# Two transformer blocks on 256 tokens: the residual and its products turned to tokens on partitions

## The chip, the cores and the metric

One core of one Trainium2 chip runs the whole program in one launch. The metric is device microseconds (us) from the first to the last instruction of an execution, the median of several executions. Inputs and outputs are float32 in HBM.

## The reference, cut to what matters

256 tokens of width 2048 (`D`) pass through two blocks. The first has two layers, the second one layer with adaptive modulation.

```
# block 1, layer i = 0, 1
h = rms_norm(x, norm_mix[i])
mix = attention(h)  (i == 0)  or  recurrent(h)  (i == 1)     # both end in a product with a 2048 x 2048 weight
x = x + mix
h = rms_norm(x, norm_ffn[i])
x = x + (silu(h @ w_gate) * (h @ w_up)) @ w_down             # 2048 -> 5632 -> 2048

# attention: qkv = h @ w_qkv (16 query heads, 4 key heads, 4 value heads of 128),
#   q, k = rope(rms_norm(head) * gain), softmax over all 256 tokens, o @ w_o

# block 2 (sh, sc, gt from c @ w_ada)
h = rmsnorm(x, g_pre_mix) * (1 + sc_m) + sh_m
proj = h @ w_in                                              # window attention and a state space model
merged = [rmsnorm(attn, g_attn_out), rmsnorm(ssm, g_ssm_out)]
x = x + (1 + gt_m) * rmsnorm(merged @ w_out, g_post_mix)
h = rmsnorm(x, g_pre_ffn) * (1 + sc_f) + sh_f
up = causal_conv(h @ w_up)                                   # 2048 -> 2 x 5632
x = x + (1 + gt_f) * rmsnorm((gelu(gate) * val) @ w_down, g_post_ffn)
```

## The kernel before

All weights, some 666 MB, are read once, in tiles of 512 KB, and every product is exact to about float32: a weight tile `wr` is split into a rounded half `wh` (a cast on ScalarE) and a rest `wl` (a subtraction on VectorE), the input into `hi` and `lo` the same way, and TensorE adds up wh·hi + wh·lo + wl·hi in PSUM. A queue on SP loads tiles up to four ahead, and the split runs up to two tiles ahead of TensorE. TensorE works through the tiles in the order of a plan (`plan_weights`). The order on each engine is that of the program text, moved by a scheduler with priorities, and an engine carries out its own list strictly in order.

There are two ways to run a tile. In `gemm` the **weight is stationary**: a tile holds four blocks of 128 input features by 256 output features; each 128 x 128 weight is loaded into the array and the tokens stream past, 512 columns for `wh` (256 tokens, `hi` and `lo` side by side) and 256 columns for `wl`. That is 8 instructions of 512 columns and 8 of 256, and the result has features on partitions. In `gemm_t` the **input is stationary**: 128 tokens by 128 features are loaded, and 512 columns of the weight stream past; a tile is 12 instructions of 512 columns, and the result has tokens on partitions. Both stream 6144 columns for each tile. Before the change only gate and up of the first two feed-forward networks (FFN) use `gemm_t`; their result is turned by transposes on TensorE (`psh`) to become the input `hc` of the down product.

The residual is kept as eight tiles `x[0..7]` of 128 features x 2 x 256 tokens. Products into the residual (`proj_x`: `wo`, `wd`, `wrout`) run in eight blocks of 256 output features. Blocks 0 and 1 run as a pair, tile by tile in turn, into both of the two PSUM buffers `pg`; the last block, 7, is `narrow`: it runs in 256-column instructions, three for each weight block, so that the result needs one addition per half. The other blocks leave two halves of 256 columns to be added to `x` by VectorE.

A norm over features is a sum over partitions here: ScalarE squares (`stat_add`), GpSimd adds up the squares, TensorE multiplies by a matrix of ones into `psn`, and the reciprocal root is taken on 128 x 256 elements by ScalarE (Ln, Exp) and VectorE. In the attention every head block needs the same (`pss`). At the two norms inside block 2, `post` and `modulate` work over the eight tiles `x[j]`; `mix`, `ff` are the products' outputs, `gg_m`, `gg_f`, `gp_m`, `gp_f` the gains, and `hh` is the split input of the next product.

Of the kernel before, what the change touches and what calls it, by code (L numbers as in the profile page):

```python
# [8 lines left out]
F32 = mybir.dt.float32  # L9
F32R = mybir.dt.float32r  # L10
AF = mybir.ActivationFunctionType
# [5 lines left out]
T = 256  # L17
# [9 lines left out]
    ("q_gain", 1), ("k_gain", 1),  # L27
# [28 lines left out]
class Build:  # L56
    def __init__(self, ctx, tc, A, stop=None):
        self.tc, self.nc, self.A, self.stop = tc, tc.nc, A, stop
# [8 lines left out]
        self.mods = {}  # L67
# [12 lines left out]
    def const(self, name, shape, dtype=F32):  # L80
        return self.cp.tile(list(shape), dtype, tag=name, name=name, bufs=1)

# [91 lines left out]
    def plan_weights(self):  # L174
# [24 lines left out]
        for b in range(12):  # L199
            add(("qkv", b), [A["wqkv"][b]], 0, 16)  # L200
# [70 lines left out]
    def gemm(self, key, xs, kbase=0, narrow=False):  # L271
# [5 lines left out]
        for bi, a, b in seq:  # L277
            wh, wl = self.next_w()
            steps = [(m, kc, xs[kc - kbase], slice(m * 128, (m + 1) * 128)) for m in range(2) for kc in range(a, b)]
            for m, kc, x, c in steps:  # L280
                if narrow:
                    self.mm3(ps[bi][:, m, 0:256], wh[:, kc - a, c], wl[:, kc - a, c], x,
                             kc == lo, kc == hi - 1)
                else:
                    self.mm(ps[bi][:, m, :], wh[:, kc - a, c], x.rearrange("p a t -> p (a t)"),
                            start=(kc == lo), stop=False)
            for m, kc, x, c in steps if not narrow else ():
                self.mm(ps[bi][:, m, 0:256], wl[:, kc - a, c], x[:, 0, :],
                        start=False, stop=(kc == hi - 1))
            self.tick()  # L290
        return ps

    def gemm_t(self, key, xs):
# [6 lines left out]
        for _, a, b in seq:  # L300
            wh, wl = self.next_w()
            for kc in range(a, b):
                for t in range(2):
                    c = slice(t * 128, (t + 1) * 128)
                    self.mm(ps[:, t, :], xs[kc][:, 0, c], wh[:, kc - a, :], start=(kc == lo), stop=False)
                    self.mm(ps[:, t, :], xs[kc][:, 1, c], wh[:, kc - a, :], start=False, stop=False)
            for kc in range(a, b):
                for t in range(2):
                    c = slice(t * 128, (t + 1) * 128)
                    self.mm(ps[:, t, :], xs[kc][:, 0, c], wl[:, kc - a, :], start=False, stop=(kc == hi - 1))  # L310
            self.tick()
# [21 lines left out]
    def stat(self, n, pairs=8):  # L333
        return {"acc": None, "n": n, "left": pairs, "sq": [], "one": False}

    def stat_add(self, s, x, direct=False):

        sq = self.slot("sq")
        if s["left"] == 1:
            for m in range(2):  # L340
                self.act(sq[:, m, :], x[:, m, :], AF.Square)
        else:
            self.act(sq, x, AF.Square)
        s["left"] -= 1
        if direct or s["left"] == 0:
            s["sq"].append(sq)
            if direct:
                self.stat_mm(s)
        elif s["acc"] is None:
            s["acc"] = sq  # L350
        else:
            self.tt(s["acc"], s["acc"], sq, ADD, eng=self.nc.gpsimd)
            if s["left"] == 1:
                a = s["acc"]
                self.tt(a[:, 0, :], a[:, 0, :], a[:, 1, :], ADD, eng=self.nc.gpsimd)
                s["one"] = True

    def stat_mm(self, s):
        if "ps" not in s:
            s["ps"], s["first"] = self.bank("psn"), True  # L360
        todo = []
        if s["acc"] is not None:
            todo = [s["acc"][:, m, :] for m in range(1 if s["one"] else 2)]
        todo += [sq[:, m, :] for sq in s["sq"] for m in range(2)]
        s["acc"], s["sq"] = None, []
        for i, sq in enumerate(todo):
            last = s["left"] == 0 and i == len(todo) - 1
            self.mm(s["ps"][:, 0:256], self.ones, sq, start=s["first"], stop=last)
            s["first"] = False

    def stat_sum(self, s, sq):

        for t in sq[1:]:
            self.tt(sq[0], sq[0], t, ADD)
        s["left"] -= len(sq)
        s["sq"].append(sq[0])
        self.stat_mm(s)

    def stat_rs(self, s, perm=False, keep_v=False):
        self.stat_mm(s)  # L380
        ps = s["ps"]
        v = self.half("v")
        src = ps[:, 0:256]
        if perm:
            self.ts(v.rearrange("p a (k i) -> p (a i) k", i=4),
                    src.rearrange("p (i k) -> p i k", i=4), 1.0 / s["n"], MUL, EPS, ADD)
        else:
            self.ts(v[:, 0, :], src, 1.0 / s["n"], MUL, EPS, ADD)
        if keep_v:
            s["epsv"] = self.half("epsv")  # L390
            self.ts(s["epsv"], v, EPS, MUL)
        s["rs"] = self.rsqrt(v, self.half("rs"))

    def rsqrt(self, v, y):

        self.act(y, v, AF.Ln)
# [1184 lines left out]
```

## Time and profile before

| | |
|---|---|
| median of 3 runs | 3280.48 us (3278.53 to 3285.55) |
| the profiled execution | 3278.88 us, span of its instructions 3277.0 us |
| granted clock of TensorE, mean | 0.985 |
| PE (matmul) busy | 3165.5 us, 97% |
| DVE (VectorE) busy | 2341.4 us, 71% |
| ACT (ScalarE) busy | 1617.5 us, 49% |
| POOL (GpSimd) busy | 628.0 us, 19% |
| DMA | 696.20 MB, 212 GB/s over the span |
| chain that ended last | PE 85%, DVE 7% |

PE is TensorE's matmul stream, and its weight loads run beside it. The chain that ended last is followed back from the last instruction, at each step to what released it. Busy shares are means over stages that differ; the time of a stage is read in the timeline, from the start of one instruction to the start of another.

### The profile page before, as it was taken

How to read it: one execution, taken by the hardware profiler on the slowest of the kernel's cores; microseconds unless marked ns; L12 is line 12 of the kernel's file. 1: busy time of each engine (PE TensorE's matmuls, PEld its weight loads, DVE VectorE, ACT ScalarE, POOL GpSimd, SP SyncE). 2: the span in 40 equal slices, each digit the busy share in tenths (PEclk: the TensorE clock that was granted, in tenths of full speed). 3: DMA queues.
4: the chain of work that ended last, by engine and by line, in shares of the span. 5: the costliest groups of instructions: out<-in, count | busy, mean ns of one | idle time of the engine just before them, and what ended most of it. 6: DMA issues, size and time to landing. Idle time of an engine off the chain costs nothing.

```text
span 3277.0 us, 47737 instructions
## 1 busy us (share of the span) xinstructions
PE 3165.5 (97%) x17912; PEld 2729.8 (83%) x17912; DVE 2341.4 (71%) x3364; ACT 1617.5 (49%) x2275; POOL 628.0 (19%) x789
## 2 busy tenths in 40 slices
PE   8999999999999988999999999999997999999997
PEld 6888888888889877888878888888886888888887
DVE  6877677756688899777776677567678766466666
ACT  5555444334444577544433444456454555455543
POOL 2101000000000043188261543251203000000001
PEclk9999999999999999999999999999997999999999
DMA  6446888978887745688787877693453556665564
GB/s 211 135 133 211 269 270 273 303 232 260 274 267 251 231 148 161 199 263 274 254 261 252 256 253 258 191 241 117 138 167 101 189 189 185 188 191 190 188 185 137
DMA packets 230744, 696.20 MB, mean 212 GB/s; under 512 B 26992, under 2 KB 35184, under 8 KB 230512
## 3 DMA queue, kind: packets, MB, share of 16 engines
q1 hardware_dynamic: 220560, 666.40, 64.2%
q0 software_dynamic: 9088, 25.18, 2.3%
q8 instruction: 140, 2.29, 0.3%
q10 hardware_dynamic: 864, 1.57, 0.1%
q14 instruction: 92, 0.75, 0.1%
HBM read 677.31 MB, written 15.73 MB: 211 GB/s over the span
## 4 chain that ended last, share of the span: by engine, by line
PE 85%; DVE 7%; issue 2%; ACT 1%; POOL 1%; DMA 1%; DVEq 0%; SPq 0%; ACTq 0%; POOLq 0%
PE pg L138 80%; DVE wl L92 2%; PE psy L138 1%; PE psc L138 1%; DMA aw<-in_wada 1%; PE pgt L138 1%; PE psh L637 1%; PE psz L138 1%; PE pso L138 1%; PE psn L138 0%; DVE x L92 0%; DVE th L764 0%; DVE aw L841 0%; ACT wh L250 0%; POOL q L92 0%
## 5 line engine op out<-in xcount | busy, mean ns | idle before, releaser
L92 DVE TENSOR_TENSOR wl<-wr,wh 128x1024 fp32r<-128x1024 f32 (+1 forms) x1068 | 1344.1, 1261 | 609.7 <-ACT wh L250 583.9
L250 ACT CAST wh<-wr 128x1024 fp32r<-128x1024 f32 (+1 forms) x1048 | 1094.3, 1044 | 1350.8 <-PE pg L138 1124.2
L138 PE MATMUL pg<-wh,xc 128*128 128x512 f32 x2816 | 703.2, 392 | 0.0
L138 PE MATMUL pg<-hc,wh 128*128 128x512 f32 (+1 forms) x2620 | 628.5, 373 | 7.9 <-DVE x L92 6.4
L138 PEld LDWEIGHTS pg<-wh,xc 128*128 128x128 f32 x2816 | 523.7, 188 | 106.9
L138 PEld LDWEIGHTS pg<-hc,wh 128*128 128x128 f32 x2620 | 459.5, 190 | 77.3 <-issue 6.6
L138 PE MATMUL pg<-hh,wh 128*128 128x512 f32 x1696 | 430.6, 396 | 9.9 <-DVE hh L101 9.4
L92 POOL TENSOR_TENSOR sq<-sq 128x512 f32<-128x512 f32 (+1 forms) x55 | 86.5, 1573 | 1806.7 <-ACT sq L115 1805.7
L841 DVE SCALAR_TENSOR_TENSOR aw<-aw,cb 128x512 f32<-128x512 f32 x384 | 284.7, 758 | 135.7 <-DMA aw<-in_wada 132.7
L138 PE MATMUL pg<-wl,xc 128*128 128x512 f32 x1408 | 377.4, 390 | 1.1 <-DVE wl L92 1.0
L138 PE MATMUL pg<-hc,wl 128*128 128x256 f32 x2368 | 368.2, 283 | 0.4 <-DVE wl L92 0.4
L138 PEld LDWEIGHTS pg<-hh,wh 128*128 128x128 f32 x1696 | 307.0, 190 | 69.2 <-issue 13.5
L138 PEld LDWEIGHTS pg<-hc,wl 128*128 128x128 f32 x2368 | 338.0, 190 | 22.6 <-DVE wl L92 1.2
L138 PEld LDWEIGHTS pg<-wl,xc 128*128 128x128 f32 x1408 | 263.9, 188 | 57.9 <-DVE wl L92 2.9
L138 PE MATMUL pg<-xc,wh 128*128 128x512 f32 x896 | 236.6, 405 | 16.1 <-ACT wh L250 8.0
L138 PEld LDWEIGHTS pg<-hh,wl 128*128 128x128 f32 x1696 | 232.4, 191 | 17.1 <-issue 0.3
L138 PE MATMUL pg<-hh,wl 128*128 128x256 f32 x1696 | 238.4, 283 | 0.0
L138 PEld LDWEIGHTS pg<-xc,wh 128*128 128x128 f32 x896 | 164.4, 191 | 52.0 <-ACT wh L250 8.0
L138 PEld LDWEIGHTS pg<-xc,wl 128*128 128x128 f32 x896 | 123.5, 193 | 11.6 <-DVE wl L92 2.5
L138 PE MATMUL pg<-xc,wl 128*128 128x256 f32 x896 | 127.4, 285 | 0.6 <-DVE wl L92 0.6
L92 DVE TENSOR_TENSOR x<-x,pg 128x512 f32<-128x512 f32 (+1 forms) x96 | 61.8, 650 | 42.8 <-PE pg L138 42.8
L101 DVE SCALAR_TENSOR_TENSOR cv<-xpad,vecs,cv 128x256 f32<-128x256 f32 x176 | 73.4, 478 | 0.0
(301 smaller groups left out, 2875.6 us busy)
## 6 DMA issues: line engine op xcount, KB each, us to landing
aw<-in_wada SPq DMA_DIRECT2D x384, 256.0 KB, 5.2
wr<-in_wg SPq DMA_DIRECT2D x176, 512.0 KB, 4.3
wr<-in_wu SPq DMA_DIRECT2D x176, 512.0 KB, 4.6
wr<-in_wd SPq DMA_DIRECT2D x176, 512.0 KB, 4.2
wr<-in_wup SPq DMA_DIRECT2D x176, 512.0 KB, 4.5
wr<-in_wrin SPq DMA_DIRECT2D x64, 512.0 KB, 4.6
wr<-in_wdn SPq DMA_DIRECT2D x64, 512.0 KB, 3.6
wr<-in_wqkv SPq DMA_DIRECT2D x48, 512.0 KB, 4.0
```

Of the source, the lines that this page charges most:

```text
L92: return (eng or self.nc.vector).tensor_tensor(out=out, in0=a, in1=b, op=op)
L101: return self.nc.vector.scalar_tensor_tensor(out=out, in0=a, scalar=s, in1=b, op0=op0, op1=op1)
L138: self.nc.tensor.matmul(out, lhsT, rhs, start=start, stop=stop, **kw)
L250: self.nc.scalar.copy(out=wh[:, :n, :], in_=wr[:, :n, :])
L637: nc.tensor.transpose(pst[:, o:o + 128], s[t][:, i:i + 128], self.ident)
L841: nc.vector.scalar_tensor_tensor(out=t, in0=t, scalar=1.0, in1=cb[i % 4], op0=MUL, op1=MUL, accum_out=part[:, i // 4, i % 4:i % 4 + 1])
```

## The change

The residual becomes two tiles `xt[0..1]` of 128 tokens x 2048 features. `qkv`, `wo`, `wd`, `wrout`, `wout2` and `wdn2` are cut into blocks 512 outputs wide and run by `gemm_t`: 408 of the weight tiles change from `gemm` to `gemm_t`, 37.5 of them from its narrow form. There are no pairs and no narrow block any more. `wrin`, the recurrent gates, `win2`, `wglu` and `wup2` still use `gemm`, since what follows them wants features on partitions.

Norms over features are now row sums: ScalarE's squares accumulate along the row (`tstat_add`), and the root is taken on 2 or 8 columns by VectorE alone, with a bit-pattern start and four Newton steps (`rsqrt`, 14 operations). Where the next product wants features on partitions, `turn` transposes on TensorE (`psx`). In the attention, RoPE and the head norms work on four heads at once with tokens on partitions, straight from PSUM; K comes first, then four blocks of Q, and V last, so all outputs `pso` stand at the end. Gains of block 2 become rows through a small transpose, a write to DRAM and a broadcast load (`make_row`, `load_row`). The input is loaded a second time, as `xt` (2 MB). The kernel stores `xt`.

```diff
         def out_gemm(key, w, k0, k1):
-            add((key, 0), [w[0], w[1]], k0, k1)
-            for j in range(2, 8):
-                add((key, j), [w[j]], k0, k1)
+            for j in range(4):
+                add((key, j), [w[j]], k0, k1, 512)
...
-        for b in range(12):
-            add(("qkv", b), [A["wqkv"][b]], 0, 16)
+        for b in range(6):
+            add(("qkv", b), [A["wqkv"][b]], 0, 16, 512)
...
+    def tstat_add(self, s, j, t, x):
+
+        sq = self.slot("sq", (128, 512))
+        self.act(sq, x, AF.Square, accum_out=s["ss"][:, 4 * t + j:4 * t + j + 1])
...
+    def rsqrt(self, v, n):
+
+        t, y = self.col(n), self.col(n)
+        self.ts(t.bitcast(I32), v.bitcast(I32), 1, ALU.logical_shift_right)
+        self.ts(y.bitcast(I32), t.bitcast(I32), -1.0, MUL, float(0x5F3759DF), ADD)
+        for _ in range(4):
+            self.tt(t, y, y, MUL)
+            self.stt(t, t, -0.5, v, MUL, MUL)
+            self.stt(y, t, 1.5, y, ADD, MUL)
+        return y
...
+    def turn(self, src, j, fn):
+
+        for q in range(2):
+            ps = self.bank("psx")
+            for f in range(2):
+                for t in range(2):
+                    o = f * 256 + t * 128
+                    i = (2 * q + f) * 128
+                    self.nc.tensor.transpose(ps[:, o:o + 128], src[t][:, i:i + 128], self.ident)
+            for f in range(2):
+                fn(4 * j + 2 * q + f, ps[:, f * 256:(f + 1) * 256])
...
         def one(j, ps):
-            self.add_ps(self.x[j], ps, j in self.NARROW)
+            for t in range(2):
+                with self.tc.high_priority(offset=200):
+                    self.tt(self.xb(j, t), self.xb(j, t), ps[:, t, :], ADD)
             if st is None:
                 return
-            self.stat_add(st, self.x[j])
+            for t in range(2):
+                self.tstat_add(st, j, t, self.xb(j, t))
             if g is not None:
-                self.split_x(j, g, xc)
-            else:
-                xc[j] = self.scale_x(j, xc[8])
-            yield
-
-        for j in [0] + list(range(2, 8)):
-            ps = self.gemm((key, j), xs, kbase, narrow=j in self.NARROW)
-            for i, p in enumerate(ps):
-                self.spawn(one(j + i, p))
+                yield
+                self.turn([self.xb(j, t) for t in range(2)], j, self.split_g(g, xc))
...
+        nc.gpsimd.dma_start(out=gn, in_=self.A["qkg"].to_broadcast([128, 512]))
...
+        def norm_rope(ps, cs):
+
+            ss = self.col(8)
+            R = []
+            for t in range(2):
+                p = ps[:, t, :].rearrange("p (h f) -> p h f", h=4)
...
+                r, u = self.slot("qr", (128, 4, 128)), self.slot("qu", (128, 4, 128))
+                self.tt(r, p, tab(0, 128), MUL)
+                self.tt(u[:, :, 0:64], p[:, :, 64:128], tab(128, 64), MUL)
+                self.tt(u[:, :, 64:128], p[:, :, 0:64], tab(192, 64), MUL)
+                sq = self.slot("qsq", (128, 4, 128))
+                self.act(sq.rearrange("p h f -> p (h f)"), ps[:, t, :], AF.Square)
+                nc.vector.tensor_reduce(out=ss[:, 4 * t:4 * t + 4], in_=sq, axis=AX.X, op=ADD)
+                self.tt(r, r, u, ADD, eng=nc.gpsimd)
+                R.append(r)
...
+            f = self.rsqrt(ss, 8)
+            for t in range(2):
+                fb = f[:, 4 * t:4 * t + 4].rearrange("p (h o) -> p h o", o=1).to_broadcast([128, 4, 128])
+                self.tt(R[t], R[t], fb, MUL)
+            return R
...
+        for j in range(4):
+            Y = []
+            for t in range(2):
+                y = self.slot("y", (128, 512))
+                self.stt(y, self.xb(j, t), st["rs"][:, t:t + 1], rows[j], MUL, MUL)
+                Y.append(y)
+            self.turn(Y, j, fn)
...
+        def one(j, ps):
+            for t in range(2):
+                m = mix[j, t]
+                self.stt(m, ps[:, t, :], sts_["rs"][:, t:t + 1], m, MUL, ADD)
+                self.tstat_add(stm, j, t, m)
+                self.tt(m, m, gg[j], MUL, eng=nc.gpsimd if j < 3 else None)
...
+    def post(self, mix, st, st2=None):
+
+        for j in range(4):
+            for t in range(2):
+                x = self.xb(j, t)
+                self.stt(x, mix[j, t], st["rs"][:, t:t + 1], x, MUL, ADD)
+                if st2 is not None:
+                    self.tstat_add(st2, j, t, x)
```

**Order on ScalarE, the first instructions.** `x` and `vecs` are the input by features and the gains, `wr` a weight tile, `xc` the split input of the first product, `sq` squares. Before:

```order
L130 ACT_TABLE_LOAD
L115 ACTIVATE sq<-x_72 128x512 [waits DMAHW0_49]
L115 ACTIVATE xc<-x_72,vecs 128x256 [waits DMAHW1_49]
L115 ACTIVATE xc<-x_72,vecs 128x256
L250 CAST wh<-wr 128x1024 [waits DMAHW2_49]
L115 ACTIVATE sq<-x_73 128x512 [waits DMAHW3_49]
L115 ACTIVATE xc<-x_73,vecs 128x256 x2
L250 CAST wh<-wr 128x1024 [waits DMAHW4_49]
```

and now:

```order
L134 ACT_TABLE_LOAD
L253 CAST wh<-wr 128x1024 [waits DMAHW2_49]
L253 CAST wh<-wr 128x1024 [waits DMAHW4_49]
L253 CAST wh<-wr 128x1024 [waits DMAHW7_49]
L119 ACTIVATE xc<-x,vecs 128x256 [waits DMAHW1_49,DMAHW0_49]
L119 ACTIVATE xc<-x,vecs 128x256
L119 ACTIVATE xc<-x,vecs 128x256 [waits DMAHW3_49]
```

Three weight casts now stand ahead of the first `xc`; the squares, now of `xt`, come after all sixteen `xc`.

**Order on TensorE, one step of the attention.** `pg` is the product with `wqkv`, `psc` the scores of a head, `pss` the sum over a head's features, `pst` transposes, `pso` a head pair's output. Before, a pair of heads came up with each block of 256 columns:

```order
L138 MATMUL psc<-q 128x256 x2
L138 MATMUL pss<-qsq,ones 128x512
L138 MATMUL pg<-xc,wh 128x512 x8
L138 MATMUL pg<-xc,wl 128x256 x8
L567 MATMUL pst<-ct,P 128x128 x8
L138 MATMUL psc<-q 128x256 x2
L138 MATMUL pg<-xc,wh 128x512 x8
L138 MATMUL pg<-xc,wl 128x256 x8
L138 MATMUL pg<-xc,wh 128x512 x8
```

and now the four heads of a block come at once, between the last instructions of a block and the first of the next:

```order
L142 MATMUL pg<-wl,xc 128x512 x2
L537 MATMUL pst<-ct,qr 128x128 x2
L142 MATMUL pg<-wl,xc 128x512
L537 MATMUL pst<-ct,qr 128x128 x6
L142 MATMUL pg<-wl,xc 128x512
L142 MATMUL pg<-wh,xc 128x512
L142 MATMUL psc<-q 128x256 x8
L142 MATMUL pg<-wh,xc 128x512 x7
L142 MATMUL pg<-wl,xc 128x512 x4
L587 MATMUL pst<-ct,P 128x128 x8
L142 MATMUL pg<-wh,xc 128x512 x8
L142 MATMUL pg<-wl,xc 128x512 x4
```

The query is now turned (`qr` into `pst`) ahead of the scores, all eight score products stand in a row, and the outputs have left this place.

**Order on TensorE, from mixer 2 to the last FFN.** `sc` is the split input of the output product, `hh` that of the next product, `psn` the sums of squares, `y` the normed residual with its row gain, `psx` its transposes, `psw` the gains turned into rows. Before:

```order
L138 MATMUL pg<-sc,wh 128x256 x2
L138 MATMUL pg<-sc,wl 128x256
L138 MATMUL psn<-sq,ones 128x256 x13
L138 MATMUL pg<-hh,wh 128x512 x9
L138 MATMUL pg<-hh,wl 128x256 x8
```

and now:

```order
L142 MATMUL pg<-wh,sc 128x512 x8
L142 MATMUL pg<-wl,sc 128x512 x4
L1071 MATMUL psw<-ct,gp_f 16x128
L1071 MATMUL psw<-ct,gg_f 16x128
L417 MATMUL psx<-ct,y 128x128 x8
L142 MATMUL pg<-hh,wh 128x512 x6
L417 MATMUL psx<-ct,y 128x128 x2
L142 MATMUL pg<-hh,wh 128x512 x3
L417 MATMUL psx<-ct,y 128x128 x6
```

The thirteen products with ones are gone, and transposes stand in their place; only the first eight of them stand ahead of the first product with `hh`.

## Rows read from the trace of the kernel before

**Rows 1.** The page, its first part: busy time by engine.

```profile
PE 3165.5 (97%) x17912; PEld 2729.8 (83%) x17912; DVE 2341.4 (71%) x3364; ACT 1617.5 (49%) x2275; POOL 628.0 (19%) x789
```

**Rows 2.** Timeline of PE, end of the attention layer's output projection: start, length, instructions.

```profile
255.38 2.00 PE L138 MATMUL pg<-hc,wh 128*128 128x512 f32 x8
...
288.90 2.00 PE L138 MATMUL pg<-hc,wh 128*128 128x512 f32 x8
...
291.69 0.40 PE L138 MATMUL pg<-hc,wh 128*128 128x256 f32 x2
...
302.85 0.40 PE L138 MATMUL pg<-hc,wh 128*128 128x256 f32 x2
```

**Rows 3.** Timeline of PE, gate and up of the first feed-forward network.

```profile
559.89 1.98 PE L138 MATMUL pg<-wh,xc 128*128 128x512 f32 x8
...
568.05 1.98 PE L138 MATMUL pg<-wh,xc 128*128 128x512 f32 x8
```

**Rows 4.** Timeline of PE, four transposes between two weight tiles.

```profile
579.67 0.60 PE L637 MATMUL psh<-ct,ga 128*128 128x128 f32 x4
...
582.91 2.00 PE L138 MATMUL pg<-hc,wh 128*128 128x512 f32 x8
```

**Rows 5.** Timeline of PE, products with ones between two weight tiles, two places.

```profile
88.05 1.02 PE L138 MATMUL pss<-qsq,ones 128*128 128x512 f32 x2
...
91.70 2.00 PE L138 MATMUL pg<-xc,wh 128*128 128x512 f32 x8
...
308.69 1.46 PE L138 MATMUL psn<-sq,ones 128*128 128x256 f32 x6
...
312.75 1.98 PE L138 MATMUL pg<-wh,xc 128*128 128x512 f32 x8
```

**Rows 6.** Lines by form, VectorE: operation, shapes, count, busy us, mean ns, idle before.

```profile
L92 DVE TENSOR_TENSOR wl<-wr,wh 128x1024 fp32r<-128x1024 f32 x1036 | 1313.5, 1270 | 585.8 <-ACT wh L250 567.0 <-PE psb L1043 11.5 <-issue 2.7
...
L92 DVE TENSOR_TENSOR x<-x,pg 128x512 f32<-128x512 f32 x84 | 57.3, 683 | 39.0 <-PE pg L138 39.0
...
L101 DVE SCALAR_TENSOR_TENSOR ga<-pg,rsc,ga 128x512 f32<-128x512 f32 x44 | 32.8, 746 | 19.9 <-PE pg L138 19.9
```

**Rows 7.** Timeline of VectorE, a chain of dependent operations on 32 columns.

```profile
918.53 0.18 DVE L98 TENSOR_SCALAR spw<-spw 128x32 f32<-128x32 f32 x1
...
919.19 0.19 DVE L92 TENSOR_TENSOR spw<-spw,spw 128x32 f32<-128x32 f32 x1
```

**Rows 8.** Timeline of PE and ACT, the first 31 us.

```profile
8.00 1.22 PE L138 MATMUL pg<-xc,wh 128*128 128x512 f32 x2 [8.00 <-ACT wh L250]
...
29.11 2.00 PE L138 MATMUL pg<-xc,wh 128*128 128x512 f32 x8
...
12.37 1.03 ACT L250 CAST wh<-wr 128x1024 fp32r<-128x1024 f32 x1
```

**Rows 9.** Waits of PE: releaser, us in total, times, longest us.

```profile
PE psc L138 <- DVE q L92: 7.4, 5, 2.2
...
PE pg L138 <- DVE x L92: 6.9, 2, 6.4
```

**Rows 10.** Timeline of PE, end of the second feed-forward network and start of mixer 2.

```profile
2155.12 0.28 PE L138 MATMUL pg<-hc,wl 128*128 128x256 f32 x1
...
2162.60 4.01 PE L138 MATMUL pg<-hh,wh 128*128 128x512 f32 x9 [4.73 <-DVE hh L101]
```

**Rows 11.** Timeline of PE, end of mixer 2 and start of the last feed-forward network.

```profile
2480.05 0.28 PE L138 MATMUL pg<-sc,wl 128*128 128x256 f32 x1
...
2515.15 4.23 PE L138 MATMUL pg<-hh,wh 128*128 128x512 f32 x9 [4.67 <-DVE hh L101]
```

**Rows 12.** Timeline of PE and VectorE, the last product and the last additions.

```profile
3257.18 0.28 PE L138 MATMUL pg<-hc,wl 128*128 128x256 f32 x1
...
3272.62 1.28 DVE L92 TENSOR_TENSOR x<-x,ff 128x512 f32<-128x512 f32 x2
```

**Rows 13.** Lines by form, ScalarE: squares of the residual.

```profile
L115 ACT ACTIVATE sq<-x 128x512 f32<-128x512 f32 x43 | 26.6, 626 | 22.5 <-DVE x L92 21.1 <-DMA x<-in_x 1.4
```

More of the change, by code (lines that the diff above doesn't have):

```diff
@@ L10 @@
 F32R = mybir.dt.float32r
+I32 = mybir.dt.int32
 AF = mybir.ActivationFunctionType
@@ L278, in gemm @@
             wh, wl = self.next_w()
[L279 to L283, printed above, removed]
-                else:
[L285 to L288, printed above, removed]
+            steps = [(m, kc, slice(m * 128, (m + 1) * 128)) for m in range(2) for kc in range(a, b)]
+            for m, kc, c in steps:
+                self.mm(ps[bi][:, m, :], wh[:, kc - a, c], xs[kc].rearrange("p a t -> p (a t)"),
+                        start=(kc == lo), stop=False)
+            for m, kc, c in steps:
+                self.mm(ps[bi][:, m, 0:256], wl[:, kc - a, c], xs[kc][:, 0, :],
                         start=False, stop=(kc == hi - 1))
@@ L355, in stat_add @@
                 self.tt(a[:, 0, :], a[:, 0, :], a[:, 1, :], ADD, eng=self.nc.gpsimd)
[L356 to L392, printed above, removed]
@@ new lines, in rs_row, with xb @@
+    def rs_row(self, s):
+        b = self.half("rsx", (128, 2, 128))
+        ps = self.bank("psr")
+        for t in range(2):
+            self.ts(b[:, t, :], self.ones, s["rs"][:, t:t + 1], MUL)
+            self.nc.tensor.transpose(ps[:, t * 128:(t + 1) * 128], b[:, t, :], self.ident)
+        s["row"] = self.half("row")
+        self.nc.scalar.copy(out=s["row"][:, 0, :], in_=ps[:, 0:256])
+    def rsb(self, s):
+        return s["row"].to_broadcast([128, 2, 256])
+    def xb(self, j, t):
+        return self.xt[t][:, 512 * j:512 * j + 512]
@@ new lines, in to_heads @@
+        def to_heads(R, out):
+            for q in range(2):
+                pst = self.bank("pst")
+                for h in range(2):
+                    for t in range(2):
+                        o = h * 256 + t * 128
+                        nc.tensor.transpose(pst[:, o:o + 128], R[t][:, 2 * q + h, :], self.ident)
+                d = self.slot("q")
+                nc.scalar.copy(out=d.rearrange("p a t -> p (a t)"), in_=pst)
+                out.append(d)
+        K, V = [], []
+        hc = [None] * 16
@@ L574, in heads, with values, outputs @@
+        def values(ps):
+            for t in range(2):
+                v = self.slot("vt", (128, 4, 128))
+                self.act(v.rearrange("p h f -> p (h f)"), ps[:, t, :], AF.Copy, scale=st["rs"][:, t:t + 1])
+                V.append(v)
+        def outputs(j):
             pso = self.bank("pso")
@@ L1099, in mixer2 @@
         hx = [None] * 16
-        for j in range(8):
-            self.modulate(st, j, xg[j], sh, hx)
+        self.modulated(st, rows, sh, hx)
         u, u4 = [None] * 4, [None] * 4
@@ L1579 @@
     o = r.results[0]["out_0_dram"]
-    return np.ascontiguousarray(o.transpose(0, 2, 1, 3).reshape(D, T).T)[None]
+    return o.reshape(1, T, D)
```

546 lines of the change are left out of this document (238 added, 308 removed).

## The prediction

> **What bounds the kernel now.** I read the page first: PE is busy for 3165.5 of 3277.0 us, DVE for 2341.4 [rows 1], at a mean granted clock of 0.985. So nearly all of the time is TensorE streaming weights at the higher of its two levels, 2.4 GHz, and some 111 us are idle. Two things can make it shorter: a cheaper weight tile, or less idle. The price of a tile I read in the timeline of PE from start to start. The idle time I took from the list of PE's waits and the timeline around the long ones: the start [rows 8], one late PSUM buffer [rows 9], the start of mixer 2 [rows 10], the change from mixer 2 to the last FFN [rows 11], and the tail [rows 12].
>
> **The weight tile.** Every tile streams 6144 columns, 2.56 us at 2.4 GHz, in whatever form. With the weight stationary, 12 tiles take 288.90 − 255.38 = 33.52 us, 2.793 each, in 16 instructions; the narrow form takes (302.85 − 291.69)/31 = 0.36 us for a weight block, 2.88 for a tile of eight, in 24 [rows 2]. With the input stationary, three tiles take 568.05 − 559.89 = 8.16 us, 2.72 each, in 12 [rows 3]. What is left over the columns is 0.233/16, 0.32/24 and 0.16/12: 13 to 15 ns for each instruction in all three forms. So the tile is dearer by its instructions alone, and the changed tiles are of a form that the trace shows on the same shapes. 370.5 wide tiles gain 0.073 each, 27.0 us; 37.5 narrow ones 0.16 each, 6.0 us. **−33.0 us.** I see no reason for either end to move by more than 2 us.
>
> The Trainium skill ("TensorE: Matmul & The Clock Gate", section "Wait — 56ns, not 53.3ns?") gives a fixed cost of about 2.5 ns for each matmul at the full clock. By that rule the 1932 instructions that fall away would be worth an estimated 4.8 us and not 33. The rows here show five times that cost, so I keep the rows.
>
> **TensorE's added and removed work.** The orders of the two kernels show 206 more transposes of 128 x 128 (96 of the residual, 64 of the normed residual `y`, 40 of queries and keys, six of gains and roots) and 12 fewer (values, roots): 194 net. Four transposes stretch a tile step from 2.793 to 582.91 − 579.67 = 3.24 us, 0.112 us each [rows 4]. The 16 that stand in waits which are costed below (the first eight at each norm of block 2) are left out: 178 × 0.112 = **+19.9 us**. The sums with ones go away. A `pss` stretches a step to 91.70 − 88.05 = 3.65, 0.86 us more than a tile; ten make **−8.6 us**. Three `psn` (six instructions in the trace) stretch a gate step to 312.75 − 308.69 = 4.06, 1.34 more; six such groups lie inside the stream, **−8.0 us** [rows 5]. The new sums over two columns number 12 and I take them as nothing. Busy time of PE in all: −29.7 us.
>
> The same page of the Trainium skill (section "Part 4: PE-mode transpose") has some 275 ns for a transpose in a kernel. An estimate by it would be 178 × 0.275 = 49 us for these, and the sum below would come out at 3252 us. The trace disagrees, with 112 ns inside the stream.
>
> **The idle time, place by place.** For the steps on DVE I take: an operation on 512 columns 0.68 us, one with a scalar 0.75, a weight rest 1.27 [rows 6]; a dependent step on a few columns (919.19 − 918.53)/3 = 0.22 [rows 7], so the 16 steps from row sums to roots take 3.5 us; on ACT a square 0.63 [rows 13], some 0.8 with its accumulator.
>
> *Start.* Now the first product stands at 8.00 and the fourth tile starts at 29.11, where three tiles alone need 8.4 [rows 8]: 12.7 us are lost over these tiles. In the new order three casts stand ahead of the first `xc`. ACT's third cast runs at 12.37 now, after squares and `xc` that no longer precede it [rows 8], so the first product should come at 14 to 17 instead of 8. After that a tile needs two slices of the input, not four, and ACT has no squares in between. I put the fourth tile 2 us earlier. If the 2 MB of `xt` hold up weights, it is 6 later; if the slices run ahead, 6 earlier. **−2 (−6 to +6).**
>
> *Attention.* A block of four query heads has eight tiles, 8 × 2.72, with 24 transposes and eight scores of some 0.43 (half of a `pss`): 27.9 us of PE. DVE in it has eight weight rests (10.2), the rotation of both halves (2.7), two reductions and two scalings (2.7), the root (3.1), four maxima and eight half-width scalings (5.5), and small ones: 25.4 us, 91%. That is close, but under PE. Waits to add are those of scores for the copies of queries on ACT, about 1.2 us (two operations of the length of a square) at each of four blocks, and 2.5 at the end, where the outputs of the first head pairs precede `wo`. Waits to lose are the five of `psc` for `q`, 7.4 us in all [rows 9], and some 3 us of others. **0 (−6 to +12).** What is queued behind a score product that waits is the rest of the weight stream, so such a wait costs its full length.
>
> *Residual blocks.* Now the third block of a product needs a PSUM buffer while two additions of the pair are late: once that stops PE for 6.4 us, 6.9 in all [rows 9]. Blocks are now 512 wide and alternate between buffers, and an addition (0.68) has a whole block, at least 21 us, before its buffer is wanted. The transposes of the last block stand one tile into the next product, which needs its slices only from the seventh tile on. I add half a us of short waits. **−7.5 (−7.5 to 0).**
>
> *Start of mixer 2.* Now 2162.60 − 2155.40 = 7.2 us [rows 10], counted from the end of the last product. Then: two additions 1.4, a square 0.8, the root 3.5, two products with rows 1.5, four transposes 0.5, `hi` and `lo` 1.0: 8.7. **+1.5 (0 to +5).** The gain rows come through DRAM; they are asked for well ahead, since the down product of 11 tiles a block hides them. Without that cover their load would add its own few us.
>
> *Mixer 2 to the last FFN.* Now 2515.15 − 2480.33 = 34.8 us [rows 11], in which squares pass through ACT, GpSimd and PE twice. Then: two updates 1.5, the last gain on DVE 1.4, a square 0.8, the root 3.5, eight updates of the residual 6.0, a square 0.8, the root 3.5, `y` 1.5, transposes 0.5, `hi` and `lo` 1.0: 20.5, say 21.5 with the handing over between engines. The next gain row needs a transpose, a write and a read; it starts with the last product and has these 15 us until `y`. **−13 (−17 to −8).**
>
> *Tail.* Now 3277.0 − 3257.46 = 19.5 us [rows 12]. Then additions 1.4, square 0.8, root 3.5, eight updates 6.0, from the last update to the end 3.1 as now, 3277.0 − 3273.9 [rows 12]: 14.8. **−4.7 (−6 to −3).** Short waits inside mixer 2: −1.
>
> **Sum.** −33.0 + 19.9 − 8.6 − 8.0 − 2 + 0 − 7.5 + 1.5 − 13 − 4.7 − 1 = −56.4. From the profiled execution's 3278.9 us that is 3222.5; the execution lies 1.6 us under the median of the three runs, so the median would be 3224. I take **3223 us**.
>
> **Rivals.**
> *A, VectorE becomes the bound in the attention.* At 91% it has 2.5 us to spare in a block, and its operations there (on views of four heads, out of PSUM) are not in the trace. Were the 15 us beside the weight rests a third to two thirds longer, it would need 30 to 35 us, and four blocks and the end would lose some 12 to 25 us: 3235 to 3248. For it: the long chain from block to scores, all on DVE and ACT. Against it: most of that work overlaps the next block's weights.
> *B, the tile gains little*, because the 13 ns come from somewhere else than the instruction and return with the wider tiles: without 28 of the 33 us, 3251. Against it speaks that gate and up show 2.72 with these very shapes [rows 3]. Transposes at twice their price give 3243.
> *C, slower.* ACT carries out its list in order. At the end of each of the 36 residual and output blocks its squares wait for additions on DVE, and the next weight casts stand behind them. If an addition comes more than 3 to 4 us after its product, the two split tiles that stand ready are used up and PE stops; at 2 us for each of 36 blocks that is +72: 3295. Against it: the additions have a raised priority, and a weight rest ahead of them takes 1.27.
>
> **How the numbers follow.** The forecast, 3205 to 3238: 0.72. A: 0.14. B: 0.06. C: 0.04 in full; a mixture that loses all the gain, within 0.2%: 0.04. The likeliest is 3223; the range takes the lower ends of the start, the attention and the gap (−14, some of it) and, upwards, A and a part of B: **3205 to 3250**. A measurement of this kernel tells about 0.2%, 6.6 us, from no change. Faster by more than that 0.92, within 0.04, slower 0.04.
>
> **What would show it.** The blocks of `wd` in 12-instruction steps of 2.72; the residual's transposes at 0.11 each; a gap of about 21 us before the last FFN and no 6 us stall in the down product; PE busy near 3136. I am wrong if DVE is busy throughout the attention with PE waiting for `q` or `qr` (A), if the steps stay near 2.79 (B), or if PE waits for `wh` from ACT at block ends (C).

## The result and the profile after

The changed kernel takes 3240.87 us (median of 4 runs, 3239.04 to 3243.99) beside 3280.81 us for the kernel before: a ratio of 0.9877, 95% interval 0.986 to 0.9895, some 40 us faster. The forecast was 3223 us, range 3205 to 3250. Run once more later, beside the experiments, it gave 3242.20 us and a ratio of 0.9874 (0.986 to 0.9887).

The page's busy line, which answers to [rows 1]:

```profile
PE 3136.0 (97%) x16104; PEld 2635.6 (81%) x16104; DVE 2224.3 (69%) x3374; ACT 1584.4 (49%) x2256; POOL 534.1 (16%) x761
```

PE is busy for 29.5 us less, beside −29.7 in the forecast. That it lies so near is luck: in the second execution the page has 3132.6, which is 33.0 less, and the experiment on the form of the tile gives 22 to 25 us for a part that the forecast had at 30. The span fell by 34.8 us in the profiled execution, so idle time fell by 5 only; the forecast had 27. The idle time is what went another way.

To see where, I cut both timelines of PE at the first product with each input (the stages below) and set the lengths against the forecast's terms, spread over the stages they belong to. (The wide tile is 0.073 us a tile, the narrow one 0.16, a transpose 0.112, a `psn` group 1.3.) The two executions of the changed kernel show what repeats.

| stage (us) | before | forecast change | after | change | after, again |
|---|---|---|---|---|---|
| attention and `wo` | 303.21 | −11.8 | 289.19 | −14.0 | 286.04 |
| FFN 0, gate and up, both halves | 489.06 | −0.6 | 487.69 | −1.4 | 487.68 |
| FFN 0, down, both halves | 249.82 | −4.7 | 243.90 | −5.9 | 243.91 |
| recurrent mixer | 251.94 | −0.4 | 250.86 | −1.1 | 251.43 |
| `wrout` | 94.45 | −0.5 | 96.04 | +1.6 | 95.90 |
| FFN 1, gate and up, first half | 272.35 | −0.4 | 280.30 | **+8.0** | 279.83 |
| FFN 1, down, first half | 148.92 | −10.4 | 146.18 | **−2.7** | 145.96 |
| FFN 1, second half, and the start of mixer 2 | 352.85 | −2.2 | 349.95 | −2.9 | 350.71 |
| mixer 2 up to `glu` | 245.72 | −0.8 | 250.87 | **+5.2** | 250.74 |
| `glu`, output product, gap to the last FFN | 106.83 | −15.6 | 91.38 | −15.4 | 91.41 |
| last FFN, up, first half | 248.68 | +2.7 | 253.87 | **+5.2** | 253.76 |
| last FFN, rest | 493.63 | −6.9 | 485.36 | −8.3 | 485.36 |
| tail | 19.54 | −4.7 | 16.61 | −2.9 | 16.57 |
| sum | 3277.0 | −56.3 | 3242.2 | −34.8 | 3239.3 |

Four stages hold the miss. PE's waits of the changed kernel (releaser, us in total, times, longest) name three of them:

```profile
PE psx L417 <- DVE y L105: 24.3, 2, 17.8
...
PE pg L142 <- DVE wl L96: 7.7, 6, 2.8
PE pg L142 <- ACT wh L253: 5.8, 1, 5.8
PE pst L537 <- DVE qr L96: 4.7, 5, 1.3
...
PE pg L142 <- DVE hh L105: 3.6, 8, 0.5
```

The waits for `x` of [rows 9] are gone, and that for `q` has become one for `qr`, 4.7 us. New is one wait of 5.8 us for a weight cast, and the six waits for `wl` have grown from 2.0 us to 7.7; 5.4 of these lie in the first down product of FFN 1. The wait for `y`, 24.3, is the two norms of block 2 (6.4 and 17.8).

What held: the tile. In the down product of FFN 0 the timeline of PE in the changed kernel reads

```profile
600.11 1.98 PE L142 MATMUL pg<-wh,hc 128*128 128x512 f32 x8
601.92 1.07 PE L142 MATMUL pg<-wl,hc 128*128 128x512 f32 x4
...
605.55 1.98 PE L142 MATMUL pg<-wh,hc 128*128 128x512 f32 x8
```

Two tiles lie between the first and the last of these: (605.55 − 600.11)/2 = 2.72 us a tile, as in [rows 3]. Eight transposes of the residual inside the stream, in `wo`:

```profile
223.88 1.03 PE L417 MATMUL psx<-ct,xt 128*128 128x128 f32 x8
...
227.51 1.98 PE L142 MATMUL pg<-wh,hc 128*128 128x512 f32 x8
```

The step with them takes 227.51 − 223.88 = 3.63 us, so each adds (3.63 − 2.72)/8 = 0.114. The gap before the last FFN, against [rows 11], again in PE's timeline:

```profile
2464.60 1.07 PE L142 MATMUL pg<-wl,sc 128*128 128x512 f32 x4
...
2483.72 2.20 PE L417 MATMUL psx<-ct,y 128*128 128x128 f32 x8 [17.83 <-DVE y L105]
2486.36 3.10 PE L142 MATMUL pg<-hh,wh 128*128 128x512 f32 x6 [0.44 <-DVE hh L105]
```

From the last product's end (2465.67) to the first with `hh` it is 20.7 us; 21.5 were forecast, 34.8 stood before.

### The profile page after: what moved, and what is told of

It is laid out like the page before. It is cut to its first block, busy times and chain, and to the rows that moved or that the text cites. A ratio compares the mean times of both kernels' runs of the same rounds, so it can differ in the third digit from the quotient of the medians.

```text
span 3242.2 us, 44027 instructions
## 1 busy us (share of the span) xinstructions
PE 3136.0 (97%) x16104; PEld 2635.6 (81%) x16104; DVE 2224.3 (69%) x3374; ACT 1584.4 (49%) x2256; POOL 534.1 (16%) x761
## 5 line engine op out<-in xcount | busy, mean ns | idle before, releaser
L96 DVE TENSOR_TENSOR wl<-wr,wh 128x1024 fp32r<-128x1024 f32 x1060 | 1343.8, 1269 | 731.3 <-ACT wh L253 696.2
L253 ACT CAST wh<-wr 128x1024 fp32r<-128x1024 f32 x1040 | 1094.3, 1052 | 1378.0 <-PE pg L142 1169.7
L142 PE MATMUL pg<-wh,xc 128*128 128x512 f32 x3200 | 802.3, 393 | 20.4 <-ACT xc L119 14.1
L142 PEld LDWEIGHTS pg<-wh,xc 128*128 128x128 f32 x3200 | 599.2, 189 | 144.2 <-ACT xc L119 14.1
L142 PE MATMUL pg<-wh,hc 128*128 128x512 f32 x2368 | 592.4, 392 | 0.0
L142 PEld LDWEIGHTS pg<-wh,hc 128*128 128x128 f32 x2368 | 444.2, 189 | 91.6
L142 PE MATMUL pg<-wl,hc 128*128 128x512 f32 x1184 | 318.0, 390 | 5.4 <-DVE wl L96 5.4
L142 PEld LDWEIGHTS pg<-wl,hc 128*128 128x128 f32 x1184 | 222.2, 188 | 52.8 <-DVE wl L96 6.4
L96 POOL TENSOR_TENSOR i<-i,xv 128x512 f32<-128x512 f32 x16 | 32.7, 2048 | 992.0 <-ACT i L123 989.6
L142 PE MATMUL pg<-xc,wh 128*128 128x512 f32 x512 | 128.7, 393 | 1.1 <-DVE wh L255 1.1
L142 PEld LDWEIGHTS pg<-xc,wh 128*128 128x128 f32 x512 | 92.0, 189 | 17.9 <-DVE wh L255 1.5
```

What stands on the lines that cost most here:

```text
L96: return (eng or self.nc.vector).tensor_tensor(out=out, in0=a, in1=b, op=op)
L142: self.nc.tensor.matmul(out, lhsT, rhs, start=start, stop=stop, **kw)
L253: self.nc.scalar.copy(out=wh[:, :n, :], in_=wr[:, :n, :])
```

## The experiments

All are edits of the changed kernel, but for one of the kernel before. Where no range is given, a time is that of one execution, and what an edit did is read from its stages.

**The form of the tile alone.** In `gemm_t`, for all products but gate and up:

```diff
+            if key[0] not in ("g", "u"):
+                st4 = [(m, kc, q) for m in range(2) for q in (m, m + 2) for kc in range(a, b)]
+                for m, kc, q in st4:
+                    self.mm(ps[:, m, :], wh[:, kc - a, q * 128:(q + 1) * 128],
+                            xs[kc - kbase].rearrange("p a t -> p (a t)"), start=(kc == lo and q == m), stop=False)
+                for m, kc, q in st4:
+                    self.mm(ps[:, m, 0:256], wl[:, kc - a, q * 128:(q + 1) * 128], xs[kc - kbase][:, 0, :],
+                            start=False, stop=(kc == hi - 1 and q == m + 2))
```

> The changed kernel, with one part put back: the tiles of qkv, wo, wd, wrout, wout2 and wdn2 are run with the weight stationary again (8 instructions of 512 columns and 8 of 256 for each tile, into the same PSUM buffers, in the same blocks of 512 outputs); what the sums hold is not the reference's. All else stays: row norms, transposes, orders. If a tile costs 13 to 15 ns for each instruction beyond its columns, as the timeline of the kernel before shows, each of 408 tiles goes from 2.72 to 2.793 us and the kernel is 30 us slower, near 3270 us, with tile steps of 2.79 in every one of these products. If the instruction count is worth only 2.5 ns for each of the 1632 instructions that come back (rival B), it is 4 us slower, near 3245, and the steps stay at 2.73.

It took 3259.93 us (3255.10 to 3266.33; ratio to the kernel before 0.9934, 0.9912 to 0.9957), some 18 us over the changed kernel's 3240.87 to 3242.20; the profiled spans (3255.3 against 3242.2 and 3239.3) differ by 13 to 16. By the page PE is busy for 21.6 us more (3157.6) and idle for 8.5 less. Neither number came out. The step did, in the same product as above:

```profile
602.60 2.00 PE L142 MATMUL pg<-hc,wh 128*128 128x512 f32 x8
604.44 1.11 PE L142 MATMUL pg<-hc,wl 128*128 128x256 f32 x8
...
608.19 2.00 PE L142 MATMUL pg<-hc,wh 128*128 128x512 f32 x8
```

(608.19 − 602.60)/2 = 2.795 us, again over two tiles. By stages: the down products of FFN 0 are longer by 6.2 us for 88 tiles and those of the last FFN by 6.4 for 88, which is 0.07 a tile; `wo` by 2.2 for 32. But the first down product of FFN 1 (48 tiles) is 1.6 shorter, and from mixer 2 through the gap (32 tiles) nothing is added. In the first of these PE waits for `wl` in the changed kernel, 5.4 us in two waits, and with slower tiles 2.0 in one: the slower tile seems to fit into the wait. But six other runs have this product at 141.5 to 142.2 us with the faster tile (they are named below), and beside those it is 2.3 to 3.1 longer, so that it fits is not shown. So 13 to 15 ns for each instruction is right, rival B is wrong, and the term was mis-sized: of the 30 us of the wide form 13 to 19 are real in this kernel, and 8.5 went into idle time. Beside the second execution of the changed kernel PE is busy for 25.0 us more. Most of what lies between 21.6 and 25.0 is the attention before `wo`: PE is busy there for 169.19 us with the form put back and for 166.14 in the second execution, both at a granted clock of 1.00, but for 169.12 in the first, at 0.99. The last 5 us I could not place. The Trainium skill's figure of about 2.5 ns for a matmul ("TensorE: Matmul & The Clock Gate", section "Wait — 56ns, not 53.3ns?") does not agree with any of these steps, where four instructions more cost 75 ns.

**The length of the root.** `for _ in range(4)` in `rsqrt` becomes 8.

> The changed kernel with eight Newton steps in place of four in every root: 12 more operations of 0.2 us on VectorE, 2.4 us for each root. It shows which roots lie on the path. If only the four roots of block 2 that nothing hides are exposed (start of mixer 2, the two between mixer 2 and the last FFN, the tail), the kernel is 9.5 us slower. If the chain on VectorE also sets the head transposes in the attention (rival A in a weak form), PE's waits for qr, 0.8 to 1.3 us at each of five blocks now, grow by 2.4 each, 12 us more: 21 us slower, near 3262. If neither is on the path, no change.

3265.02 us, span 3263.2: 21.0 longer, the number that was expected, but by luck: the parts below add up to 27.3, and FFN 1 up to the end of its first down product was 6.8 shorter in this run, which the edit does not explain. The four roots of block 2 gave 2.4 (start of mixer 2), 4.7 (gap) and 2.3 (tail), 9.4 as reckoned. The attention grew by 17.9, more than the five waits. The scheduler moved the heads' steps later past the products, so that the last block of queries came after the end of the last product, in PE's timeline:

```profile
186.50 2.05 PE L537 MATMUL pst<-ct,qr 128*128 128x128 f32 x8 [9.47 <-DVE qr L96]
...
195.47 0.72 PE L587 MATMUL pst<-ct,P 128*128 128x128 f32 x4 [1.06 <-DVE P L100]
...
201.08 7.68 PE L142 MATMUL pso<-PT,vt 128*128 128x256 f32 x24 [1.26 <-ACT vt L119]
```

So the attention's chain on VectorE has little room before it sets the pace. With three steps:

> The changed kernel with three Newton steps in place of four, 0.6 us less for each root (in e4_newton8 four more cost 17.9 us up to wo and 9.4 us at the four roots of block 2). The four roots of block 2 then give 2.4 us. In the attention the waits for qr, 0.8 to 1.3 at five blocks, fall by up to 0.6 each: 2 to 3 us. Together 4 to 5 us; if the root is not on the attention's path below four steps, 2.4.

3238.36 us, span 3236.3. The waits for `y` fell from 24.3 to 22.5 us (at the gap from 17.8 to 16.6) and the tail by 0.6, together the 2.4 reckoned for the four roots. But the waits for `qr` stayed at 0.8 to 1.3: the scheduler places the transposes as much earlier as the chain is shorter. Up to `wo` it took 188.57 us, between the 190.49 and 187.34 of two executions of the changed kernel, so no gain in the attention can be told.

**The wait for a cast in FFN 1.** ScalarE's, GpSimd's and PE's timelines of the changed kernel around it:

```profile
1376.19 1.05 ACT L253 CAST wh<-wr 128x1024 fp32r<-128x1024 f32 x1 [0.53 <-ACT xc L119]
1387.74 0.63 ACT L123 ACTIVATE cb<-cb 128x512 f32<-128x512 f32 x1 [10.50 <-DMA cb<-in_c]
...
1389.95 1.03 ACT L253 CAST wh<-wr 128x1024 fp32r<-128x1024 f32 x1
...
1368.40 0.51 POOL L1075 DMA_DIRECT2D d_gpm<-rowt  x1 [62.19 <-ACT rowt L1073]
...
1374.24 0.62 POOL L96 TENSOR_TENSOR yr<-bi,sv 128x256 f32<-128x256 f32 x1 [2.56 <-DMA bi<-in_bpk]
...
1380.84 2.20 POOL L821 DMA_DIRECT2D cb<-in_c  x4
...
1384.11 1.07 PE L142 MATMUL pg<-wl,xc 128*128 128x512 f32 x4
1391.03 3.78 PE L142 MATMUL pg<-wh,xc 128*128 128x512 f32 x8 [5.85 <-ACT wh L253]
```

ScalarE has nothing to do with squares here. It stands 10.5 us before a SiLU of `cb`, the conditioning vector for the second modulation task, whose load GpSimd issues only at 1380.84. That load stands behind GpSimd's first work for the state space model, part of which waits for loads, and that in turn behind the write of a gain row (`d_gpm`, `make_row`), which is new with the change: GpSimd stands 62.19 us before it, until TensorE and ScalarE have turned the row at the end of `wrout`. Weight casts are queued behind the SiLU. PE runs dry at 1385, waits 5.9 us, and its next eight instructions take 3.78 us in place of 1.98. In the kernel before, GpSimd's timeline has that load ahead of this work and of its loads:

```profile
1383.31 2.17 POOL L821 DMA_DIRECT2D cb<-in_c  x4
...
1386.60 0.54 POOL L1002 DMA_DIRECT2D bi<-in_bpk  x1
```

The edit holds the SiLU back:

```diff
-            self.nc.scalar.copy(out=wh[:, :n, :], in_=wr[:, :n, :])
+            self.cast = self.nc.scalar.copy(out=wh[:, :n, :], in_=wr[:, :n, :])
...
-        for _ in range(3 if c0 else 2):
+        for _ in range(10 if c0 else 2):
...
-            self.act(t, t, AF.Silu)
+            i = self.act(t, t, AF.Silu)
+            if c0:
+                self.after(i, self.cast)
```

> The changed kernel with the SiLU of the second modulation task (cb) held back on ScalarE by some ten steps of that task, behind the weight casts that are issued by then. If PE's wait of 5.9 us for wh at 1391 is ScalarE standing before cb, whose load GpSimd issues late behind its own work, the gate and up stage of the second FFN goes from 280.3 us to 271 to 273, as before the change. If the casts are late for the squares at the end of wrout (rival C), the wait and the 280 us stay.

3230.82 us, span 3229.0, and the stage takes 271.72 us: 8.6 less. The wait is gone, so rival C is not what happened. That the write of the gain row is what made the load late is read from the timeline; no run moves it.

**The first down product of FFN 1.** Both kernels lose time here, the one before 8 us and the changed one 5 to 9, as will be seen. In the changed one, VectorE's timeline:

```profile
1677.01 1.07 DVE L841 SCALAR_TENSOR_TENSOR aw<-aw,cb 128x512 f32<-128x512 f32 x1 [3.67 <-DMA aw<-in_wada]
...
1683.07 2.46 DVE L841 SCALAR_TENSOR_TENSOR aw<-aw,cb 128x512 f32<-128x512 f32 x1
...
1687.01 1.80 DVE L841 SCALAR_TENSOR_TENSOR aw<-aw,cb 128x512 f32<-128x512 f32 x1
...
1689.94 2.73 DVE L96 TENSOR_TENSOR wl<-wr,wh 128x1024 fp32r<-128x1024 f32 x1
...
1693.62 2.31 DVE L96 TENSOR_TENSOR wl<-wr,wh 128x1024 fp32r<-128x1024 f32 x1
...
1698.77 2.48 DVE L841 SCALAR_TENSOR_TENSOR aw<-aw,cb 128x512 f32<-128x512 f32 x1
...
1704.40 0.68 DVE L841 SCALAR_TENSOR_TENSOR aw<-aw,cb 128x512 f32<-128x512 f32 x1
...
1705.62 1.21 DVE L96 TENSOR_TENSOR wl<-wr,wh 128x1024 fp32r<-128x1024 f32 x1
```

VectorE stands 3.7 us before an `aw` tile that has not landed, with weight rests queued behind; then each operation takes 1.1 to 2.7 us while GpSimd works (0.68 and 1.21 for the same ones from 1704 on, when GpSimd's arithmetic is through), and `wl` comes late. Without the multiplications (in `ada_task`, `if not c0:` ahead of the operation, and `part` set to zero):

> The changed kernel without the 136 multiplications of VectorE for the last 34 columns of the modulation vector (aw; the loads stay, the sums are set to zero). If the two waits of PE for wl in the second down product (2.6 and 2.8 us, at 1692 and 1702) come from VectorE being overloaded by aw beside GpSimd, that product goes from 146.2 to some 138 us. If they come from the additions into the residual at the block's end, which stay, it keeps 146. The wait for wh at 1391 stays in both, as ScalarE still waits for cb.

3236.28 us, span 3234.5; the product takes 136.87 us, 9.3 less, and PE is busy for all of it. The windows of the product, in the changed kernel and without `aw` (length, busy time of PE, PEld, DVE, ACT and POOL, then the granted clock, the DMA engines' share and GB/s):

```profile
1647.98:1794.16 146.18, 140.83 (x733) 114.05 (x732) 100.53 (x136) 55.60 (x63) 56.66 (x80) 0.98 0.78 256
1648.83:1785.70 136.87, 136.87 (x733) 111.96 (x732) 74.45 (x70) 55.61 (x63) 61.23 (x80) 1.00 0.83 273
```

Of the 9.3 us, 5.35 are PE's idle time; the other 3.96 are the same 733 instructions taking longer at a granted clock of 0.98. And 9.3 is the most that `aw` costs: six other runs that leave it alone (`e2_silu`, `e4_newton8`, `e5_hh`, `e6_start`, `e10_start2`, `e11_newton3`) show 141.5 to 142.2 us for this product, so beside these it is some 5. Why the changed kernel itself shows 146 in both executions is open. The edit takes away the stand before the load and the slow operations together; which of the two costs more is open, and no run takes GpSimd's work away. The same edit in the kernel before:

> The kernel before without the same 136 multiplications of VectorE (the loads stay, the sums are set to zero). My prediction laid the wait of 6.4 us at 1702 to the pair of blocks that leave two additions for one PSUM buffer. If that is right, the wait stays, at 4 us or more, and the down product keeps about 149 us. If VectorE is overloaded by aw, the wait goes and the product takes 141 us or less.

3273.38 us, span 3271.6; the product takes 140.50 us, 8.4 less, and the 6.4 us are gone. PE's waits of that kernel:

```profile
PE pg L138 <- DVE x L92: 1.0, 2, 0.6
```

So the pair of blocks alone was not the cause. What released PE was an addition, but the addition was late behind `aw` and the weight rests, as VectorE's timeline of the kernel before shows; PE went on at 1702.59:

```profile
1690.43 1.18 DVE L841 SCALAR_TENSOR_TENSOR aw<-aw,cb 128x512 f32<-128x512 f32 x1 [3.63 <-DMA aw<-in_wada]
...
1701.77 0.68 DVE L92 TENSOR_TENSOR x<-x,pg 128x512 f32<-128x512 f32 x1
```

To spread `aw` thinner (`self.pace = 0.56` for 0.61):

> The changed kernel with the aw multiplications of the second modulation task paced at 0.56 for each tile in place of 0.61. If it is only the density of aw beside GpSimd's work that overloads VectorE in the second down product, that product goes from 146.2 to 140 to 143 us and nothing comes back elsewhere: 3 to 6 us less. If VectorE is full there either way, the waits move by a tile or two and the time stays within 2 us.

3244.35 us, span 3242.6. The product took 141.45 us, but the six runs named above, which leave the pace alone, show 141.5 to 142.2, and the next gate and up grew by 2.6, with a wait for `wl` there. Nothing is gained by spreading alone.

**The starts of block 2.** Eight tiles from the first `hh` on take 30.3 us in the last FFN, 25.2 before. With `y` made ahead (`normed(j)` makes `y` of block `j`; its definition is left out here, and so is the loop that it replaces):

```diff
...
+        normed(0)
+        self.turn(Y[0], 0, fn)
+        normed(1)
+        normed(2)
+        self.turn(Y[1], 1, fn)
+        normed(3)
+        self.turn(Y[2], 2, fn)
+        self.turn(Y[3], 3, fn)
```

> The changed kernel with the normed residual y of the next blocks made one block ahead at both norms of block 2, so that their transposes can stand earlier in TensorE's order. If the 2.3 us that each start costs beyond its 24 transposes (30.2 us for eight tiles after the gap, 25.2 before the change) is the wait for hh, 0.4 to 0.5 us at each block, the eight tiles take some 28 us and the kernel is 3 to 4 us faster. If it is the transposes themselves, nothing changes.

3233.30 us, span 3231.5. Mixer 2 up to `glu` fell from 250.9 (250.7 in the second execution) to 246.3 us. The eight tiles of the last FFN fell to 28.9, but the output product and gap before them were 1.5 longer, so that place gained nothing; `e2_silu`, without this edit, has 29.1 there. In mixer 2 the eight tiles take 27.9 us, beside 29.1 and 30.6 in the two executions of the changed kernel and 24.1 before: 1.3 to 2.7 us gained. Beside the first execution the other 3.3 us lie in the part of mixer 2 from its first product with `ac` to `glu`, which the edit does not touch and whose time goes with the granted clock. The windows of that part (columns as above), of the changed kernel's first and second execution, of the kernel before, and of the kernel before without `aw`, whose edit does not reach here:

```profile
2320.97:2394.98 74.01, 73.19 (x586) 63.84 (x586) 37.97 (x51) 30.39 (x50) 9.95 (x10) 0.95 0.53 167
2321.47:2392.20 70.73, 69.91 (x586) 60.78 (x586) 38.56 (x51) 30.40 (x50) 9.95 (x10) 1.00 0.57 175
2333.95:2408.32 74.37, 71.38 (x651) 64.20 (x649) 45.78 (x54) 31.95 (x53) 8.78 (x6) 1.00 0.46 142
2324.24:2403.24 79.00, 76.09 (x650) 68.61 (x649) 45.87 (x54) 31.95 (x53) 8.77 (x6) 0.94 0.43 134
```

With this edit it takes 70.73 us at 1.00. So 3.3 to 4.6 us of a difference in mixer 2 can be the clock alone, and of the 3 to 4 us expected from the edit 1.3 to 2.7 are seen, at one of the two places.

**The kernel's start.** Dependencies put two, two and four inputs ahead of the first three casts (`self.first` holds the sixteen inputs `xc` in ScalarE's order):

```diff
+            if i < 3:
+                self.after(self.cast, self.first[(1, 3, 7)[i]])
```

> The changed kernel with the first eight inputs of ScalarE's order put between the first three weight casts (two ahead of the first cast, two ahead of the second, four ahead of the third). The first product then starts at 8 to 9 us in place of 14.1, and the fourth tile at 21 to 23 in place of 25.9. If TensorE sets the pace of the attention, wo starts 3 to 4 us earlier; if VectorE's chain sets it, the waits for qr take it back and wo starts at most 1.5 us earlier.

3243.35 us. The first product stood at 6.99, the fourth tile at 16.99, but `wo` at 190.23, no gain. PE's timeline shows why:

```profile
6.99 3.45 PE L142 MATMUL pg<-wh,xc 128*128 128x512 f32 x8 [6.99 <-ACT wh L253]
...
16.99 1.98 PE L142 MATMUL pg<-wh,xc 128*128 128x512 f32 x8
...
21.74 2.11 PE L142 MATMUL pg<-wh,xc 128*128 128x512 f32 x8 [1.87 <-ACT wh L253]
...
28.57 3.78 PE L142 MATMUL pg<-wh,xc 128*128 128x512 f32 x8 [3.82 <-ACT wh L253]
```

The early start runs into weights that have not come: the DMA engines move some 400 GB/s without a break from 12 to 28 us, 12.4 MB in 40 us. So the same order was tried again, now with `xt` loaded later:

> The order of e6_start (the first product at 7 us), and the two loads of xt, 1 MB each, moved behind the eighth and the tenth weight tile in SP's queue, their squares with them. In e6_start the early start was given back in waits for weights, 1.9 and 3.8 us, with the DMA engines busy throughout the first 28 us at some 400 GB/s. If the 2 MB of xt take the bandwidth, the waits for wh go and wo starts 4 to 5 us earlier than in the changed kernel, at 185 to 186.5. If VectorE's chain in the attention takes the gain, the first block of queries starts earlier, but wo stays at 189 or later.

3238.84 us. The first product stands at 8.04, the waits for weights behind it fall to 0.4 us, and 5.3 us of waiting for `qr` at the first head block stand in their place: the root over the row sums of `xt` is needed there. `wo` starts at 188.33, within what the unchanged kernel shows (187.3 to 190.5). In these two runs the 2 MB more take back what the order gains, once as late weights and once as a late root.

**All together.** Held-back SiLU, `y` ahead, three steps, late `xt`:

> The changed kernel with four of these edits at once: the SiLU of cb held back (e2_silu), y made a block ahead (e5_hh), three Newton steps, and the start of e10_start2. If the losses lie apart from each other, their gains add up: 8.6, some 4, 4 to 5 and 3 to 5 us under the changed kernel's stages, 3218 to 3224 us. If VectorE's load in the second down product and in the attention ties them together, 3226 to 3232.

> The changed kernel once more, beside the kernel before and e12_best on the same chip. 3238 to 3244 us.

3224.76 us (3223.25 to 3230.98; ratio 0.9825, 0.981 to 0.984) against 3242.20 us (0.9874, 0.986 to 0.9887) on the same chip. It is just above the 3218 to 3224 us of gains that add up. In the profile, 8.1 of the 18 us come from FFN 1's gate and up, 3.8 from mixer 2 (half of it in the first eight tiles) and 4.1 from the gap with the stage after it, against the second execution of the changed kernel.

## Why the prediction was right, and where it was off

The direction, the range and the bound were right: the gap (−14.1 for −13), the start of mixer 2 (+1.8 for +1.5), the chain of the root and a transpose inside the stream (0.114 us for 0.112) came as worked out. PE's own time did too as a sum, with luck, since its first term was too large. The size was off by 18 us, in these steps:

- **The weight tile, −33.** Right for each instruction, mis-sized as a sum: the form put back costs 13 to 19 us, not 30. I multiplied the gain by all tiles, also in stages where VectorE or a load sets the pace. "I see no reason for either end to move by more than 2 us" was the wrong sentence.
- **Residual blocks, −7.5.** The step failed. I read "pg waits for x" as a buffer conflict of the pair. The stall belonged to VectorE, held up by `aw` loads and slow while GpSimd works; it came back as waits for `wl`. Taking `aw` out removes it in both kernels: −8.4 in the one before, and in the changed one −9.3, of which 4.0 are products at a lower granted clock, or some −5 beside the six other runs.
- **Not in the sum: +8.0 in FFN 1.** In GpSimd's new order the load of `cb` stands behind the write of a gain row, for which GpSimd waits 62 us, and behind work that waits for loads; that delayed, through ScalarE's order, the weight casts. The forecast asked only whether the rows arrive in time, not what is queued behind their write. Rival C had the mechanism (casts behind a waiting instruction) with the wrong instruction; delaying the SiLU gave the 8.6 us back.
- **Transposes at the two norms of block 2.** Eight tiles take 30.3 us for 25.2 in the last FFN and 29.1 for 24.1 in mixer 2, where 24 transposes account for 2.7; the rest is waits for `hh` of 0.4 to 0.5 us and tiles that the transposes break up.
- **Tail, −4.7.** It was −2.9. From the last update to the end 5.3 us pass, not 3.1: the eight updates take 5.39 us together, and 2 MB are stored behind them, as the DMA view of the end (3222 to 3243 us) shows:

```profile
GB/s 0 0 0 0 0 0 0 0 0 0 0 0 0 0 0 0 0 0 0 0 0 230 390 347 289 226 219 308 367 398 390 250 250 219 113 0 0 0 0 0
...
out_dram<-xt ACTq DMA_DIRECT2D x4, 256.0 KB, 3.4
out_dram<-xt SPq DMA_DIRECT2D x4, 256.0 KB, 3.6
```

  Each store takes 3.4 to 3.6 us to land (2.0 to 2.1 before, where the additions were slower and the stores spread out).
- **Attention, 0.** Attention and `wo` gained 14.0 to 17.2 us for a forecast of 11.8: the fourth tile starts at 25.93, 3.2 us earlier for 2, and waits of 10.4 us for `q` and `v` gave way to 6.8 for `qr` and `vt`. Rival A was near but did not decide: VectorE is busy for 22.65 of 29.0 us in a block of heads (110 to 139 us), 78%, less than the 91% of 27.9 us that I had added up.

## What to carry to other kernels

Price a cheaper instruction stream only over the stages that run at its pace; where another engine ends the waits, the gain turns into waiting. A wait's releaser is the last of a queue: look at what stood before it in that engine's order (a load, a slow neighbour) before laying the wait to a buffer. Put the granted clock beside each stage before laying a few us of it to an edit. When a change adds work to a side queue, follow every load that is issued behind it to the engine that stands still for it.

## What was not expected of the hardware

After the same wait of 2.07 us for `vt`, the same 24 instructions took 7.13 us in one execution and 5.45 in another; the granted clock is 0.81 in the window of the one and 1.00 in that of the other, the lower mean holding some time at the 1.2 GHz level. PE's timelines and the windows, of the first and of the second execution:

```profile
183.71 7.13 PE L142 MATMUL pso<-PT,vt 128*128 128x256 f32 x24 [2.07 <-ACT vt L119]
...
182.00:191.00 9.00, 7.29 (x26) 6.12 (x27) 1.98 (x5) 7.11 (x15) 0.00 (x0) 0.81 0.18 58
```

```profile
182.24 5.45 PE L142 MATMUL pso<-PT,vt 128*128 128x256 f32 x24 [2.07 <-ACT vt L119]
...
179.00:188.00 9.00, 6.93 (x36) 5.86 (x35) 2.98 (x6) 8.42 (x17) 0.00 (x0) 1.00 0.30 96
```

So one profile tells the time up to `wo` (190.49 and 187.34 us in these two) to some 3 us and no better.
